# A hybrid decoder layer on one core: the order of work around the fifth attention visit

## The chip, the core and the metric

The kernel runs on one core of one Trainium2 chip. The core has five engines that each work through their own instructions in order: TensorE (PE in the profile, its weight loads PEld), VectorE (DVE), ScalarE (ACT), GpSimd (POOL) and SyncE (SP), which here only issues DMAs. Matmuls write PSUM banks of 128 partitions x 512 f32; everything else lives in SBUF. Engines wait for each other by semaphores. The metric is the device time of one execution, in microseconds (us); less is better.

## The reference, cut to what matters

One layer of a decoder trunk, 256 tokens, width 1024, float32. One combined projection of the normed input feeds two kinds of heads; both outputs go through w_out, then a gated feed-forward part follows.

```python
proj = rms_norm(x, attn_norm_g) @ w_in
y_moba = merge_heads(moba_attention(rope(mq), rope(mk), mv))     # 8 heads of 64, causal
log_a  = log_sigmoid(gate_lr @ w_gate_up + b_gate) / 16
og     = gla_attention(gq, gk, gv, log_a)                        # 4 heads, keys 64, values 128, chunks of 64
og     = og * rsqrt(mean(og * og) + EPS) * gla_norm_g
y_gla  = merge_heads(og) * silu(gr)
x = x + concat([y_moba, y_gla]) @ w_out
h = causal_dwconv(rms_norm(x, ffn_norm_g) @ w_ffn_up, conv_w, conv_b)
x = x + (silu(h_gate) * h_val) @ w_ffn_down
out = rms_norm(x, final_norm_g)
```

With 256 tokens there is one key block, so the first kind of head ("m_" in the code) is plain causal softmax attention.

## The kernel before

**Matmuls in three parts.** Every f32 weight is split by ACT into a rounded part `hi` (L99) and by DVE into the rest `lo` (L102); activations are split likewise (`mh`, `ml`). A product is three matmuls (`mm3`, L115 to L118). Weights come in slots of 128x2048: slots 0 to 15 are w_in, 16 to 19 w_out (L141 to L143), then the up-projection. `raw` has a ring of 4 buffers, `hi` and `lo` of 3. In the plan, `(hi, n, p)` and `(lo, n, p)` split half p (1024 columns) of slot n. `lo` of a slot's last piece issues the DMA of a later slot (`load_next`, L103), on SP's queue.

**Steps and visits.** The projection runs as steps q = 0 to 47, each one group of columns and one slice of k: v is in steps 24 to 31, gv in 32 to 39, r (the gate) in 40 to 47; a step of these is two times three matmuls of 512 columns, for two token tiles. Steps 48 to 63 are the output projection: phase 0 (48 to 55) takes the heads' half y_moba with slots 16 and 17, phase 1 (56 to 63) y_gla with slots 18 and 19; each step makes 128 output columns j with 12 matmuls of 256 columns. The attention's work is put into this stream by a table (L669 to L692): `on(q, f)` runs f ahead of step q, and at q + 0.5 in its middle. What f emits lands on each engine's queue in the order written, so **the table sets the order of work on PE, ACT and DVE at once**. The attention visits PE four times for scores (29, 33.5, 36.5, 40.5); the fifth visit, at 45.5, is what the change's name speaks of.

**What the names do.** `m_scores(pr)` makes scores of two heads in two PSUM banks (and the products of GLA level pr + 2 beside them); `m_max`, `m_exp`, `m_div` (L586 to L608) are the softmax on DVE and ACT, the last of them dividing by the sums: reciprocals on DVE (L603), a 128-wide scale on ACT (L604), a 256-wide one on ACT (L606) or DVE (L608). Heads 0 to 3 are transposed on DVE (`p_blocks`, L566) and by 20 small DMAs into `pt4` (`p_turn`, L569 to L584, on SP's and POOL's queues by turns); heads 4 to 7 on PE into two PSUM banks, from which ACT copies `pt` (`m_pt`, L610 to L625). `lvl_u`, `lvl_u64` (L365) and `lvl_d_` (L402) build GLA's inner products level by level into `ATd`; `lvl_join` (L416) copies them to `AT` on ACT; `lvl_last` (L420) makes the last products on PE, `lvl_last_d` (L438) reads them on ACT. `mv_evac` and `gv_evac` (L523, L448) take v and gv out of PSUM on ACT. `m_av` (L627) and `g_av` (L454) are the products with the values; `m_av` ends with `mh`/`ml` (L643, L645). `g_tail` (L481) norms GLA's output and gates it with silu(r): L471, L477, L452, L491. `g_out` (L493) turns the result on PE (L499) and splits it (L503, L504).

**PSUM banks.** Two pools of four: `acc` for the projections, `att` for the attention, each handed out in turn. `m_av(0)` gets the `att` bank that the first half of `m_pt(3)` wrote, `m_av(1)` the second; `m_pt(3)` gets the banks of `m_scores(3)`, which `lvl_d_(5)` reads last. The output projection's four banks are, in turn, those of gv (two) and those of r (two); output column j uses bank j % 4.

Of the kernel before, what the change touches and what calls it, by code (L numbers as in the profile page):

```python
# [34 lines left out]
def trunk_kernel(ctx: ExitStack, tc: tile.TileContext, xT_d, wG_d, w5_d, wo_d, up_d, dn_d,  # L35
# [79 lines left out]
    def mm3(out, sh, sl, mh, ml, first, last, **kw):  # L115
        T.matmul(out, sh, mh, start=first, stop=False, **kw)  # L116
        T.matmul(out, sh, ml, start=False, stop=False, **kw)  # L117
        T.matmul(out, sl, mh, start=False, stop=last, **kw)  # L118
# [482 lines left out]
    def m_div(h):  # L601
        mx, pe = st["mx", h], st["pe", h]
        V.reciprocal(mx[:, 6:8], mx[:, 4:6])  # L603
        A.activation(pe[:, 0:128], pe[:, 0:128], AF.Copy, scale=mx[:, 6:7])  # L604
        if h in (2, 3, 4, 5):
            A.activation(pe[:, 128:384], pe[:, 128:384], AF.Copy, scale=mx[:, 7:8])  # L606
        else:
            V.tensor_scalar(pe[:, 128:384], pe[:, 128:384], mx[:, 7:8], None, op0=ALU.mult)  # L608
# [41 lines left out]
    def on(q, f, *a):  # L650
        plan.setdefault(q, []).append((f, a))
# [11 lines left out]
    def do(*fs):  # L663
        for f, *a in fs:
            f(*a)
# [3 lines left out]
    for q, f in (  # L669
            (2, lambda: do((xsplit, 6), (xsplit, 7), (xsq, 3), (galloc, 6), (ghi, 6), (glo, 6), (ghi, 7), (glo, 7))),  # L670
            (4, lambda: do((xadd, 3), (xsum,), (hi, 6, 0), (lo, 6, 0), (g_wgs_hi,), (hi, 7, 0))),
            (12, lambda: do((xnorm, lambda: slots[7].split_lo(0, 512)), (lambda: slots[7].split_lo(512, 1024),), (g_evac, 0), (g_lr_split,), (g_evac, 1), (g_wgs_lo,), (hi, 7, 1), (lo, 7, 1))),
            (12.5, lambda: do((DMA.dma_start, lvl, lvl_d), (masks,))),
            (13.5, lambda: do((hi, 8, 0))),
            (14.5, lambda: do((g_transpose_lr,), (g_transpose, 0), (g_transpose, 1), (xrow,), (lo, 8, 0), (g_diag,))),
            (15.5, lambda: do((g_gate_mm,), (g_gate,), (hi, 9, 0), (g_decay,), (lo, 9, 0), (hi, 9, 1))),
            (16.5, lambda: do((lvl_u, 0), (lo, 9, 1), (lvl_u, 1))),
            (18, lambda: do((rope_a, 0, 0), (rope_b, 0, 0), (hi, 10, 0), (lo, 10, 0), (rope_a, 0, 1), (rope_b, 0, 1), (hi, 10, 1), (lo, 10, 1))),
            (20, lambda: do((hi, 11, 0), (lo, 11, 0), (hi, 11, 1), (lvl_keep,), (DMA.dma_start, glag, gla_g_d))),
            (24, lambda: do((lvl_u, 2), (rope_a, 1, 0), (rope_b, 1, 0), (lo, 11, 1), (rope_a, 1, 1), (rope_b, 1, 1), (hi, 12, 0), (lo, 12, 0), (g_diag2, 0), (g_diag2, 4))),  # L680
            (29, lambda: do((hi, 12, 1), (lvl_first,), (m_scores, 0), (m_max, 0), (m_exp, 0), (m_max, 1), (m_exp, 1), (lvl_d_, 0), (lvl_d_, 1), (lvl_u, 3), (m_div, 0), (m_div, 1), (lvl_d_, 2), (lo, 12, 1), (hi, 13, 0), (lo, 13, 0))),
            (33.5, lambda: do((hi, 13, 1), (m_scores, 1), (m_max, 2), (m_exp, 2), (m_max, 3), (m_exp, 3), (lvl_u, 4), (m_div, 2), (m_div, 3), (lo, 13, 1), (lvl_d_, 3), (mv_evac, 0), (mv_evac, 1), (hi, 14, 0), (lo, 14, 0))),
            (36.5, lambda: do((hi, 14, 1), (m_scores, 2), (m_max, 4), (m_exp, 4), (m_max, 5), (m_exp, 5), (lvl_u, 5), (m_div, 4), (m_div, 5), (lvl_d_, 4), (p_blocks,), (p_turn,), (lo, 14, 1))),
            (37, lambda: do((hi, 15, 0))),
            (40.5, lambda: do((hi, 15, 1), (m_scores, 3), (m_pt, 2), (m_max, 6), (m_exp, 6), (m_max, 7), (m_exp, 7), (lo, 15, 0), (lvl_u64,), (lvl_d_, 5), (m_div, 6), (m_div, 7), (lvl_join,), (lo, 15, 1))),
            (41, lambda: do((gv_evac, 0), (gv_evac, 1), (hi, 16, 0), (lo, 16, 0))),
            (42, lambda: do((hi, 16, 1), (lo, 16, 1))),
            (45.5, lambda: do((m_pt, 3), (lvl_last,), (lvl_last_d,), (m_av, 0), (m_av, 1), (g_av, 0), (g_av, 1), (hi, 17, 0), (lo, 17, 0), (hi, 17, 1), (lo, 17, 1))),
            (48, lambda: do((g_tail,), (hi, 18, 0), (lo, 18, 0), (hi, 18, 1), (lo, 18, 1))),
            (51, lambda: do((g_out,),)),  # L690
            (52, lambda: do((A.preload_act_table_set, "abs_reciprocal_sqrt_and_small"), (hi, 19, 0), (lo, 19, 0), (hi, 19, 1), (lo, 19, 1)))):
        on(q, f)  # L692

# [49 lines left out]
    def emit(q):  # L743
        for f, a in plan.get(q, []):
            f(*a)
# [53 lines left out]
    def hsum(n):  # L799
        V.tensor_add(sqs[:, 0:2], sqs[:, 0:2], sqs[:, n:n + 2])  # L800

    for q in range(48, 64):
        ph, j = divmod(q - 48, 8)
        emit(q)
        if q == 56:
            ctx.enter_context(tc.manual_schedule())
        o = wacc[j % 4][:, (j // 4) * S:(j // 4 + 1) * S]
        h_, l_ = slots[16 + 2 * ph + j // 4].view(512)
        cs = slice((j % 4) * 128, (j % 4 + 1) * 128)
        for kk in range(4):  # L810
            if kk == 2:
                emit(q + 0.5)
            k = 4 * ph + kk
            mm3(o, h_[:, kk, cs], l_[:, kk, cs], st["mh"][:, k], ml[:, k],
                ph == 0 and kk == 0 and j < 4, ph == 1 and kk == 3, skip_group_check=True)
        if ph == 1:
            if j == 0:
                ap_.close()
                ff = ctx.enter_context(tc.tile_pool(name="ffn", bufs=1, reuse_waits="tile"))
                sqs = ff.tile([128, KT, S], F32, name="sqs", tag="big")  # L820
            if j % 4 == 0:
                ups[j // 4].alloc()
            hT = xT
            piece = (j % 4 * 512, j % 4 * 512 + 512) if j < 6 else None
            if piece:
                ups[j // 4].split_hi(*piece)
            V.tensor_add(hT[:, j], o, xT[:, j])
            A.activation(hh_[:, j], hT[:, j], AF.Copy, scale=par[:, P_FG + j:P_FG + j + 1])
            if piece:
                ups[j // 4].split_lo(*piece)  # L830
            V.scalar_tensor_tensor(hl_[:, j], hT[:, j], par[:, P_FG + j:P_FG + j + 1], hh_[:, j],
                                   op0=ALU.mult, op1=ALU.subtract)
            if j in (4, 6):
                hsum(j - 2)
            A.activation(sqs[:, j], hT[:, j], AF.Square)
# [377 lines left out]
```

## Time and profile before

| | |
|---|---|
| median of three timed runs | 309.67 us (309.52 to 310.79) |
| the profiled execution | 309.44 us, of it span 307.7 us |
| granted TensorE clock, mean | 0.991 |
| PE waiting for ACT at L637 | 2.9 us, once |
| ACT waiting for PE at L99 | 31.2 us, 11 times |
| DMA over the span | 57.10 MB, mean 186 GB/s |

The span runs from the first to the last instruction; the rest of the execution's time lies around it. Times in the rows below count from the span's start. A row of the timeline has the start, the duration, the engine, the line, the operation, the tiles written and read, and in brackets how long the engine had been idle and what released it; `x4` merges four instructions. `PEclk` is the granted TensorE clock as a share of full speed.

### The profile page before, as it was taken

How to read it: one execution, taken by the hardware profiler on the slowest of the kernel's cores; microseconds unless marked ns; L12 is line 12 of the kernel's file. 1: busy time of each engine (PE TensorE's matmuls, PEld its weight loads, DVE VectorE, ACT ScalarE, POOL GpSimd, SP SyncE). 2: the span in 40 equal slices, each digit the busy share in tenths (PEclk: the TensorE clock that was granted, in tenths of full speed). 3: DMA queues.
4: the chain of work that ended last, by engine and by line, in shares of the span. 5: the costliest groups of instructions: out<-in, count | busy, mean ns of one | idle time of the engine just before them, and what ended most of it. 6: DMA issues, size and time to landing. Idle time of an engine off the chain costs nothing.

```text
span 307.7 us, 6219 instructions
## 1 busy us (share of the span) xinstructions
PE 297.8 (97%) x2446; PEld 282.0 (92%) x2446; DVE 249.7 (81%) x464; ACT 207.0 (67%) x382; POOL 11.0 (4%) x31
## 2 busy tenths in 40 slices
PE   8999999999699999999999999999999999999992
PEld 8999988778489999999999999999999999999991
DVE  3888989969568498799999998888887788876652
ACT  4988999797978487667766776555566655534362
POOL 3010100007000000000000000000000000000000
PEclk9999999999989999999999999999999999999998
DMA  6997745254753533892666666548787722220003
GB/s 177 389 343 307 293 165 218 91 197 77 255 184 135 228 112 136 333 413 75 208 214 229 260 236 232 190 163 225 199 221 230 273 70 68 68 70 0 2 11 126
DMA packets 24188, 57.10 MB, mean 186 GB/s; under 512 B 12976, under 2 KB 14848, under 8 KB 19936
## 3 DMA queue, kind: packets, MB, share of 16 engines
q1 hardware_dynamic: 23696, 56.22, 52.2%
q0 software_dynamic: 320, 0.36, 0.6%
q8 instruction: 19, 0.31, 0.4%
q10 hardware_dynamic: 144, 0.13, 0.1%
q14 instruction: 9, 0.07, 0.1%
HBM read 53.89 MB, written 1.05 MB: 179 GB/s over the span
## 4 chain that ended last, share of the span: by engine, by line
PE 77%; ACT 9%; DVE 8%; issue 3%; DMA 1%; SPq 0%; DVEq 0%; ACTq 0%
PE att L116 14%; PE att L117 14%; PE att L118 14%; PE acc L116 9%; PE acc L117 9%; PE acc L118 9%; PE att L784 3%; DVE lo L102 3%; ACT hi L99 3%; ACT qs L512 2%; PE acc L765 1%; DMA raw<-in_w 1%; PE att L637 1%; DVE ATd L409 1%; DVE pe L590 1%
## 5 line engine op out<-in xcount | busy, mean ns | idle before, releaser
L102 DVE TENSOR_TENSOR lo<-raw,hi 128x1024 fp32r<-128x1024 f32 (+4 forms) x89 | 93.6, 1066 | 15.0 <-ACT hi L99 14.7
L99 ACT ACTIVATE hi<-raw 128x1024 fp32r<-128x1024 f32 (+4 forms) x87 | 79.9, 942 | 37.1 <-PE att L117 31.2
L116 PE MATMUL att<-hh,hi 128*128 128x256 f32 x352 | 98.4, 279 | 0.0
L117 PE MATMUL att<-hl,hi 128*128 128x256 f32 x352 | 98.3, 279 | 0.0
L118 PE MATMUL att<-hh,lo 128*128 128x256 f32 x352 | 98.2, 279 | 0.0
L116 PEld LDWEIGHTS att<-hh,hi 128*128 128x128 f32 x352 | 66.2, 188 | 0.0
L117 PEld LDWEIGHTS att<-hl,hi 128*128 128x128 f32 x352 | 66.2, 188 | 0.0
L118 PEld LDWEIGHTS att<-hh,lo 128*128 128x128 f32 x352 | 66.2, 188 | 0.0
L911 DVE SCALAR_TENSOR_TENSOR c<-us,par,c 128x256 f32<-128x256 f32 x88 | 40.7, 482 | 4.1 <-ACT c L903 2.5
L903 ACT ACTIVATE c<-us,par 128x256 f32<-128x256 f32 x44 | 24.0, 591 | 24.4 <-DVE us L893 18.9
L118 PE MATMUL acc<-dhi,gl 128*128 128x512 f32 (+1 forms) x88 | 32.2, 365 | 0.0
L117 PE MATMUL acc<-dlo,gh 128*128 128x512 f32 (+1 forms) x88 | 32.2, 365 | 0.0
L116 PE MATMUL acc<-dhi,gh 128*128 128x512 f32 (+1 forms) x88 | 31.9, 363 | 0.0
L853 DVE TENSOR_TENSOR dlo<-draw,dhi 128x1024 fp32r<-128x1024 f32 x22 | 26.7, 1219 | 0.0
L848 ACT ACTIVATE dhi<-draw 128x1024 fp32r<-128x1024 f32 x22 | 23.0, 1046 | 0.0
L893 DVE TENSOR_TENSOR us<-att,rb 128x512 f32<-128x512 f32 x20 | 13.8, 689 | 11.2 <-PE att L118 11.2
L116 PE MATMUL acc<-hi,ah 128*128 128x512 f32 x48 | 19.5, 406 | 0.0
L118 PE MATMUL acc<-hi,al 128*128 128x512 f32 x48 | 19.0, 396 | 0.0
L117 PE MATMUL acc<-lo,ah 128*128 128x512 f32 x48 | 19.0, 395 | 0.0
L117 PEld LDWEIGHTS acc<-dlo,gh 128*128 128x128 f32 x88 | 16.5, 188 | 2.0
L116 PEld LDWEIGHTS acc<-dhi,gh 128*128 128x128 f32 x88 | 16.5, 188 | 1.9
L118 PEld LDWEIGHTS acc<-dhi,gl 128*128 128x128 f32 x88 | 16.5, 187 | 1.9
(236 smaller groups left out, 517.5 us busy)
## 6 DMA issues: line engine op xcount, KB each, us to landing
raw<-in_up SPq DMA_DIRECT2D x22, 1024.0 KB, 5.0
draw<-in_dn SPq DMA_DIRECT2D x22, 512.0 KB, 5.7
raw<-in_w SPq DMA_DIRECT2D x7, 1024.0 KB, 6.0
raw<-in_wo SPq DMA_DIRECT2D x4, 1024.0 KB, 6.6
raw<-in_w SPq DMA_DIRECT2D x4, 512.0 KB, 6.4
raw<-in_wG SPq DMA_DIRECT2D x3, 528.0 KB, 5.2
raw<-in_w SPq DMA_DIRECT2D x4, 256.0 KB, 4.9
xg<-hB SPq DMA_DIRECT2D x16, 64.0 KB, 6.1
```

Source lines behind the costliest of these rows:

```text
L99: A.activation(self.hi[:, a:b], self.raw[:, a:b], AF.Copy)
L102: V.tensor_sub(self.lo[:, a:b], self.raw[:, a:b], self.hi[:, a:b])
L116: T.matmul(out, sh, mh, start=first, stop=False, **kw)
L117: T.matmul(out, sh, ml, start=False, stop=False, **kw)
L118: T.matmul(out, sl, mh, start=False, stop=last, **kw)
L512: A.activation(qs[a:a + 32], st["qk"[which]][n][b:b + 32], AF.Copy)
L784: T.matmul(st["G"][tt][c][:, :c1 - c0], sta[:, k, tt * 128:(tt + 1) * 128], mov[:, kk, c0:c1], start=k == 0 and i == 0, stop=k == KT - 1 a ...
L848: A.activation(hi, downs[i][0], AF.Copy)
L853: V.tensor_sub(lo, d, hi)
L893: V.tensor_tensor(u[:, :, 2:], upo[i][2].rearrange("p (a t) -> p a t", a=2), rb[:, None, :].to_broadcast([128, 2, S]), op=ALU.mult)
L903: A.activation(cv[i][:, a], u[:, a, 2:], AF.Identity, bias=par[:, P_CB + m:P_CB + m + 1], scale=par[:, P_CW + 2 * 2 * NP + m:P_CW + 2 * 2 ...
L911: V.scalar_tensor_tensor(c[:, a], u[:, a, w:w + S], par[:, wc:wc + 1], c[:, a], op0=ALU.mult, op1=ALU.add)
```

## The change

The table's entries from 33.5 to 51 get another order, the 256-wide division of heads 6 and 7 goes from DVE to ACT, and phase 0 of the output projection takes its output columns in the order 0, 1, 4, 5, 2, 3, 6, 7.

```diff
-        if h in (2, 3, 4, 5):
+        if h >= 2:
             A.activation(pe[:, 128:384], pe[:, 128:384], AF.Copy, scale=mx[:, 7:8])
...
-            (33.5, lambda: do((hi, 13, 1), (m_scores, 1), (m_max, 2), (m_exp, 2), (m_max, 3), (m_exp, 3), (lvl_u, 4), (m_div, 2), (m_div, 3), (lo, 13, 1), (lvl_d_, 3), (mv_evac, 0), (mv_evac, 1), (hi, 14, 0), (lo, 14, 0))),
-            (36.5, lambda: do((hi, 14, 1), (m_scores, 2), (m_max, 4), (m_exp, 4), (m_max, 5), (m_exp, 5), (lvl_u, 5), (m_div, 4), (m_div, 5), (lvl_d_, 4), (p_blocks,), (p_turn,), (lo, 14, 1))),
+            (33.5, lambda: do((hi, 13, 1), (m_scores, 1), (m_max, 2), (m_exp, 2), (m_max, 3), (m_exp, 3), (lvl_u, 4), (m_div, 2), (m_div, 3), (lo, 13, 1), (lvl_d_, 3), (hi, 14, 0), (lo, 14, 0))),
+            (36.5, lambda: do((hi, 14, 1), (mv_evac, 0), (mv_evac, 1), (m_scores, 2), (m_max, 4), (m_exp, 4), (m_max, 5), (m_exp, 5), (lvl_u, 5), (m_div, 4), (m_div, 5), (lvl_d_, 4), (p_blocks,), (p_turn,), (lo, 14, 1))),
             (37, lambda: do((hi, 15, 0))),
-            (40.5, lambda: do((hi, 15, 1), (m_scores, 3), (m_pt, 2), (m_max, 6), (m_exp, 6), (m_max, 7), (m_exp, 7), (lo, 15, 0), (lvl_u64,), (lvl_d_, 5), (m_div, 6), (m_div, 7), (lvl_join,), (lo, 15, 1))),
-            (41, lambda: do((gv_evac, 0), (gv_evac, 1), (hi, 16, 0), (lo, 16, 0))),
-            (42, lambda: do((hi, 16, 1), (lo, 16, 1))),
-            (45.5, lambda: do((m_pt, 3), (lvl_last,), (lvl_last_d,), (m_av, 0), (m_av, 1), (g_av, 0), (g_av, 1), (hi, 17, 0), (lo, 17, 0), (hi, 17, 1), (lo, 17, 1))),
+            (40.5, lambda: do((hi, 15, 1), (m_scores, 3), (m_pt, 2), (m_max, 6), (m_exp, 6), (m_max, 7), (m_exp, 7), (lo, 15, 0), (m_div, 6), (m_div, 7), (lo, 15, 1), (lvl_u64,), (lvl_d_, 5))),
+            (41, lambda: do((gv_evac, 0), (gv_evac, 1), (lvl_join,))),
+            (46, lambda: do((m_pt, 3), (lvl_last,), (lvl_last_d,), (hi, 16, 0), (lo, 16, 0), (m_av, 0), (m_av, 1), (hi, 16, 1), (lo, 16, 1), (g_av, 0), (g_av, 1), (hi, 17, 0), (lo, 17, 0), (hi, 17, 1), (lo, 17, 1))),
             (48, lambda: do((g_tail,), (hi, 18, 0), (lo, 18, 0), (hi, 18, 1), (lo, 18, 1))),
-            (51, lambda: do((g_out,),)),
+            (51.5, lambda: do((g_out,),)),
...
     for q in range(48, 64):
         ph, j = divmod(q - 48, 8)
+        j = j if ph else (0, 1, 4, 5, 2, 3, 6, 7)[j]
```

On ACT, between the exponentials of heads 6 and 7 and the copies out of m_pt(3)'s banks (L623), the rows are these (- before, + with the change; L604 and L606 divide, L449 is gv_evac, L417 and L418 are lvl_join, L99 is hi of slot 16):

```order
 L597 ACTIVATE pe_152,mx<-pe_152,mx 128x256
-L604 ACTIVATE pe_152<-pe_152,mx 128x128 x2
+L604 ACTIVATE pe_152<-pe_152,mx 128x128
+L606 ACTIVATE pe_152<-pe_152,mx 128x256
+L604 ACTIVATE pe_152<-pe_152,mx 128x128
+L606 ACTIVATE pe_152<-pe_152,mx 128x256
+L449 ACTIVATE gv<-acc,rsx 128x512 x2
 L417 ACTIVATE ATf<-ATd 64x8x64
 L418 ACTIVATE ATf<-ATd 64x8x64
-L449 ACTIVATE gv<-acc,rsx 128x512 x2
-L99 ACTIVATE hi<-raw 128x1024 x2
 L623 ACTIVATE pt<-att 128x2x64
```

Two 256-wide divisions came to ACT, gv's evacuation went ahead of the join, and both halves of hi(16) left; they now stand behind lvl_last_d, the second of them behind mh.

On DVE, behind the maxima of heads 6 and 7 (L590), the first L102 is lo(15,0), the second lo(15,1), and L368, L369 begin lvl_u64:

```order
 L590 ISA mx 128x1
 L102 TENSOR_TENSOR lo<-raw,hi 128x1024
+L603 RECIPROCAL mx<-mx 128x2 x2
+L102 TENSOR_TENSOR lo<-raw,hi 128x1024
 L368 TENSOR_TENSOR gqT<-gqT,dec_132 128x8x32
 L369 TENSOR_TENSOR gkT<-gkT,dec_132 128x8x32
```

The reciprocals came from behind the last masks to directly behind lo(15,0), and lo(15,1) from behind the divisions to behind the reciprocals.

On PE, between g_av and g_out, L116 to L118 with `acc<-hi,ah` are the projection and with `acc<-mh,hi` the output projection:

```order
 L117 MATMUL acc<-lo,ah 128x512
 L118 MATMUL acc<-hi,al 128x512
-L116 MATMUL acc<-hi,ah 128x512
-L117 MATMUL acc<-lo,ah 128x512
-L118 MATMUL acc<-hi,al 128x512
+L116 MATMUL acc<-mh,hi 128x256
+L117 MATMUL acc<-ml,hi 128x256
+L118 MATMUL acc<-mh,lo 128x256
+L116 MATMUL acc<-mh,hi 128x256
+L117 MATMUL acc<-ml,hi 128x256
+L118 MATMUL acc<-mh,lo 128x256
```

Three matmuls of the projection left this place; they now run ahead of m_pt(3). Six more of the output projection stand ahead of g_out, which comes half a step later. The new order of output columns does not show in such rows, since all of them read alike.

## The prediction

> **What bounds the kernel now.** I read the page's busy table first, then who waited for whom, then the chain of work that ended last between 66 and 92 us, then the timelines of TensorE (PE), ScalarE (ACT) and VectorE (DVE) around it.
>
> ```profile
> span 307.7 us, 6219 instructions
> PE 297.8 (97%) x2446; PEld 282.0 (92%) x2446; DVE 249.7 (81%) x464; ACT 207.0 (67%) x382; POOL 11.0 (4%) x31
> ```
>
> PE is busy 97% of the span; only what makes PE stand or run slowly is worth anything. The view of waits (idle in total, times, longest) has one long wait of PE in the whole program:
>
> ```profile
> PE att L637 <- ACT pt L624: 2.9, 1, 2.9
> ```
>
> The timeline shows it (start, duration, idle before and what released it). L617 turns the last two heads' probabilities (m_pt(3)), L435 ends lvl_last, L637/L638 are m_av, L463/L461 g_av; L116 then resumes the projection and, from 93.37, the output projection.
>
> ```profile
> 78.27 0.59 PE L617 MATMUL att<-ident,pe 64*128 64x64 f32 x12
> ...
> 79.51 0.22 PE L435 MATMUL att<-q,gkT 64*64 64x64 f32 x2
> 82.65 0.66 PE L637 MATMUL att<-pt,mv 128*64 128x256 f32 x4 [2.92 <-ACT pt L624]
> ...
> 83.35 0.65 PE L637 MATMUL att<-pt,mv 128*64 128x256 f32 x4
> ...
> 86.92 1.32 PE L463 MATMUL att<-gv,ATf 128*128 128x128 f32 x8
> 88.08 0.39 PE L461 MATMUL att<-gv,AT 128*128 128x128 f32 x2
> ...
> 89.79 0.48 PE L116 MATMUL acc<-hi,ah 128*128 128x512 f32 x1
> ...
> 93.37 0.28 PE L116 MATMUL acc<-mh,hi 128*128 128x256 f32 x1
> ...
> 97.66 0.71 PE L499 MATMUL att<-ident,y 64*128 64x64 f32 x16
> ```
>
> The chain says why (start, length, what):
>
> ```profile
> 74.04 1.14 DVE lo L102
> ...
> 76.45 0.41 DVE ATd L409 x2
> ...
> 77.86 0.63 ACT ATf L417
> ...
> 79.14 1.14 ACT gv L449 x2
> 80.28 1.89 ACT hi L99 x2
> 82.17 0.16 ACT pt L623
> 82.33 0.28 ACT pt L624
> ```
>
> m_av(0) takes the PSUM bank that m_pt(3) filled. It comes free when ACT has read it (L623, L624), and ACT, which works in order, first does the join of the masks, gv's evacuation and both halves of hi(16). PE was done with lvl_last at 79.73 (79.51 + 0.22) and stood until 82.65.
>
> The wait has a second price. Four stretches follow; the columns are the length, busy time and instructions of PE, PEld, DVE, ACT and POOL, the granted clock, the DMA share, GB/s:
>
> ```profile
> 77.00:80.40 3.40, 2.73 (x66) 2.01 (x64) 1.88 (x4) 3.30 (x7) 0.46 (x4) 1.00 0.49 79
> 80.40:83.80 3.40, 1.15 (x13) 0.98 (x15) 2.36 (x2) 3.38 (x10) 0.00 (x0) 1.00 0.96 395
> 83.80:87.20 3.40, 3.40 (x23) 2.73 (x20) 0.82 (x3) 1.66 (x8) 0.00 (x0) 0.51 1.00 407
> 87.20:90.60 3.40, 3.40 (x28) 3.26 (x29) 2.69 (x3) 3.37 (x12) 0.00 (x0) 0.99 0.23 89
> ```
>
> PE is idle for 2.25 of the 3.40 us from 80.40, and the next 3.40 run at a granted clock of 0.51. The stretch from 77.00 had 0.67 idle, and the clock stayed at 1.00 behind it.
>
> **The change, part by part.** The sum stands against the profiled execution: 309.44 us, of which the span is 307.7; the median of the three timed runs, 309.67, is 0.23 above it.
>
> *mv's evacuation behind hi(14).* From the timelines of PE and ACT:
>
> ```profile
> 69.39 0.67 PE L398 MATMUL att<-gqT,gkT 64*64 64x32 f32 x32
> ```
>
> ```profile
> 63.09 1.27 ACT L524 ACTIVATE mv<-acc,rsx 128x512 f32<-128x512 f32 x2
> 64.24 2.01 ACT L99 ACTIVATE hi<-raw 128x1024 fp32r<-128x1024 f32 x2
> 66.80 0.40 ACT L597 ACTIVATE e<-e,mx 128x128 f32<-128x128 f32 x1 [0.55 <-DVE mx L590]
> ...
> 76.96 0.88 ACT L604 ACTIVATE pe<-pe,mx 128x128 f32<-128x128 f32 x2 [1.91 <-DVE mx L603]
> ```
>
> With hi(14) first, DVE's lo(14,0) and the maxima behind it start 1.15 us sooner, and ACT's idle 0.55 before the exponentials goes: the exponentials of heads 4 and 5, p_blocks, and the exponentials of heads 6 and 7 all come 0.55 earlier. PE does not wait there, so this earns nothing by itself. ACT has read mv's banks by 66.2 (63.09 + 2.01 + 1.14). PE writes them anew three matmuls ahead of L398 at 69.39, that is at 68.7 (0.239 each: 15 from 89.79 to 93.37), so the later read costs nothing either.
>
> *Divisors behind the exponentials, all on ACT.* Now ACT stands 1.91 us before L604 at 76.96, since the reciprocals are behind the level of 64 and the masks on DVE. What the two forms cost on ACT stands earlier in the chain, for heads 2 and 3:
>
> ```profile
> 61.68 0.29 ACT pe L604
> 61.97 0.40 ACT pe L606
> ```
>
> lo(15,0) ends at 75.18 (74.04 + 1.14), less 0.55 is 74.65; two reciprocals take it to 74.85. ACT's four instructions (two of 0.29, two of 0.40: 1.4) end at 76.2, and gv's evacuation (1.14) at 77.35. DVE meanwhile does lo(15,1) (1.14, to 76.0), the level of 64 (75.18 to 76.45 in the chain, 1.27, to 77.25) and the last masks (0.41, to 77.65). The join waits for these and takes two of 0.63: 78.9. The two 0.40 are new on ACT; they lie in the 1.91 that it now idles. All of this is beside the projection on PE.
>
> *Three matmuls ahead of m_pt(3), hi(16) behind lvl_last_d.* L617 starts 0.7 later, at 79.0, and ends at 79.6. Its banks were read by the last masks until 77.65, so it need not wait. From 79.6 ACT, free since 78.9, reads it (0.16 + 0.28 for the first bank, done at 80.05). lvl_last ends on PE at 80.43 (79.73 + 0.7). So the bank is free 0.4 us before PE asks: **the wait of 2.92 goes**. If ACT were later than I have it, the cover is those 0.4 us and then each us costs one. The three matmuls only change place, and hi(16) goes into ACT's idle time further down.
>
> What is late next? m_av(0) also reads pt4, which the small DMAs of p_turn fill (count, duration, first and last issue; landing):
>
> ```profile
> L584 SPq DMA_DIRECT2D pt<-tb x4: 599/612/624, 74.9 to 77.5; - x4
> DMA to landing us min/median/max: 1.9/2.7/3.7
> ```
>
> The last is issued at 77.5, so it lands between 79.4 and 81.2; 0.55 earlier, since p_blocks is, that is 78.85 to 80.65 against 80.43. The wait is 0 to 0.25, and 0.8 if the DMAs do not come earlier at all. I take 0, by the median (79.65). On SP's queue the next two loads of w_out stand behind these DMAs, and stay there; the load that lo(16) releases leaves later, which is priced below.
>
> *The clock.* m_av is four pieces of 0.70 at full clock (82.65 to 83.35), 2.80. g_av is 24 matmuls of 0.107 (16 from 88.08 to 89.79), 2.57. From 82.65 to 89.79 the two took 7.14, so the slow clock cost 1.77; by the clock itself it is 3.40 x 0.49 = 1.67. I take **1.7**. With at most 0.7 us of idle in it, as in the stretch from 77.00, the clock should hold.
>
> [...]
>
> *The output banks and g_out.* The output projection then starts at 93.37 - 2.92 - 1.7 = 88.8. At 0.119 a matmul (36 from 93.37 to 97.66), three and a half steps of 12 take 5.0: PE comes to g_out, where it now stands, at 93.8. Is y ready? Rows of ACT, then of DVE:
>
> ```profile
> 84.62 0.72 ACT L643 ACTIVATE mh<-att 128x256 fp32r<-128x256 f32 x3
> 87.03 0.60 ACT L643 ACTIVATE mh<-att 128x512 fp32r<-128x512 f32 x1 [1.69 <-PE att L638]
> ...
> 89.41 0.27 ACT L471 ACTIVATE e<-att 128x128 f32<-128x128 f32 x1
> ...
> 94.02 1.26 ACT L452 ACTIVATE gr<-acc,rsx 128x512 f32<-128x512 f32 x2
> ```
>
> ```profile
> 88.60 2.36 DVE L102 TENSOR_TENSOR lo<-raw,hi 128x1024 fp32r<-128x1024 f32 x2 [0.26 <-ACT hi L99]
> ...
> 94.74 1.29 DVE L491 TENSOR_TENSOR y<-y,gr 128x512 f32<-128x512 f32 x2 [0.18 <-ACT gr L452]
> ```
>
> On ACT, L623 at 82.17 to L643 at 84.62 are 2.45; from 79.6 that is 82.1. Then hi(16,0) 0.95, mh 1.3 (0.72 + 0.60), three halves of hi 2.85: L471 at 87.2, against 89.41 now 2.2 earlier. DVE's last lo ends at 82.1 + 0.95 (hi) + 1.14 (lo) + 1.3 (ml, taken like mh) + 3 x 1.14 = 88.9, against 90.96 (88.60 + 2.36) 2.0 earlier. So y is ready at 96.03 (94.74 + 1.29) - 2.0 = 94.0, its first half at 93.4. PE reaches g_out at 93.8, and its first eight turns (0.35) need only the first half: a wait of 0 to 0.3, I take **0.1**. PE's lead was 4.6, that of y is only 2.0: this is the thinnest place. The new order of banks keeps a second wait away: the banks of r are now asked for in the fifth step, at 95.2; without it the third step would ask at 91.6, and ACT frees the first at 92.4 (94.02 + 0.63 - 2.2). The splits of slot 17, wanted at 91.6, end at 88.9.
>
> *Loads and the rest.* The first up-weights are loaded when lo(16) ends, at 86.7 (82.1 + 0.95 + 1.14 + 1.3 + 1.14, rounded), and first used by ACT at the second row:
>
> ```profile
> raw<-in_up SPq DMA_DIRECT2D x22, 1024.0 KB, 5.0
> ```
>
> ```profile
> 105.49 0.63 ACT L99 ACTIVATE hi<-raw 128x512 fp32r<-128x512 f32 x1 [2.67 <-PE acc L117]
> ```
>
> ACT waits there for PE, not for a load; 4.5 earlier is 101.0, 14 us after the issue, against 5.0 to landing. hi(19) must now wait for slot 16 until the end of PE's sixth step, 98.0, and its lo ends at 101.1; PE wants it in the thirteenth, at 106.4. The view of waits has no row of PE behind g_out, so what it wins it keeps.
>
> The sum: 2.92 + 1.7 - 0.1 = **4.5 us**; 309.44 - 4.5 = 304.9, or 305.2 beside the median.
>
> **The rivals.**
> 1. *The wait moves to pt4's DMAs.* For it: the slowest landing, 81.2 unshifted. Price 0.25 to 0.8, no slow clock (0.67 idle left it alone): 305.4 to 306.0. Against it: the median landing.
> 2. *The slow clock stays* though the gap goes, since m_av's narrow matmuls bring it on, not the gap. For it: it set in some 1.2 us after PE had resumed, on L637. Against it: the stretch ahead of it is the only one here with over 2 us of idle. Price 1.7: 306.9. [...]
> 3. *g_out takes over.* If y is not 2.0 but 0 to 1 us earlier, it comes at 95.0 to 96.0; PE waits 0.9 to 1.9 for its second half and, near the top, may lose the clock (1.7): 306.0 to 308.7. For it: hi(16) and hi(17) now stand ahead of the norms without a gap. Against it: the sum above, from rows.
> 4. *Slower.* The same place, one mechanism: ACT, with three of the four halves of hi(16) and hi(17) between m_av and the norms, holds y back beyond where it is now, 96.03. From a gap of 2.8 at g_out (y at 96.9) with two slow stretches behind it (3.4) the loss is 6.2, more than the 4.6 won and the 1.55 of half a per cent: 311.3 and up. Against it: those halves start 2 us earlier than now and are no longer.
> 5. *It does not do what it says:* the join or the reads before m_av stay late, and PE waits as now: 309.7. That takes 2.9 us on ACT or DVE that I overlook.
>
> **How the numbers follow.** Forecast 304.5 to 305.4: 0.68. First rival 0.12, second 0.07, third 0.06, fourth 0.03, fifth 0.04. The likeliest gives 305.2. Forecast and first rival hold 0.80 and reach 306.0; with the price of the clock, the larger of the unknowns, the range is 304.4 to 306.9. Over 0.5% (1.55 us, about what a measurement of this kernel can tell from no change) faster is below 308.1: forecast, first, second and most of the third, 0.92; within it a rest of the third and the fifth, 0.05; slower 0.03.
>
> **What would show it.** In the changed profile: no wait of PE at L637 over 0.3 us; granted clock 1.00 from 80 to 90; the output projection at 88.8 (93.37 now); g_out at 93.8 with under 0.3 idle; the span near 303.2. A wait at L637 put down to a DMA speaks for the first rival, a 0.5 clock without a gap for the second, a wait at L499 for the third. The forecast is wrong if PE's lead at 88.8 is not there, or is gone by 98.

## The result and the profile after

The changed kernel takes 306.07 us, the median of six runs (305.88 to 306.49); the kernel before, run beside it, 309.61 (six runs, 308.54 to 310.79). The ratio is 0.9885, with a 95% interval of 0.9861 to 0.9908: faster by 1.15%, about 3.5 us of the 4.5 that were forecast. The profiled executions took 309.44 and 306.01.

The page of the changed kernel, its span, PE's busy row and the share of each engine in the chain that ended last:

```profile
span 303.9 us, 6219 instructions
...
PE 296.2 (97%) x2446; PEld 280.6 (92%) x2446; DVE 248.6 (82%) x462; ACT 207.7 (68%) x384; POOL 11.5 (4%) x31
...
PE 95%; DMA 1%; ACT 1%; SPq 0%; issue 0%; DVE 0%; ACTq 0%
```

The span is 3.8 us shorter. PE still sets the end, and 95% of the chain is now PE's own work. Its waits (idle in total, times, longest):

```profile
PE att L637 <- ACT pt L624: 0.6, 1, 0.6
PE acc L764 <- ACT hi L99: 0.3, 1, 0.3
```

The wait at L637 fell from 2.9 to 0.6 us; the forecast had it gone. (The 0.3 at L764 lies near 6 us, at the start of the program, far from the change.) The timeline of the changed kernel on PE, ACT and DVE at the places that the prediction named:

```profile
78.98 0.59 PE L617 MATMUL att<-ident,pe 64*128 64x64 f32 x12
...
80.21 0.23 PE L435 MATMUL att<-q,gkT 64*64 64x64 f32 x2
81.01 0.66 PE L637 MATMUL att<-pt,mv 128*64 128x256 f32 x4 [0.58 <-ACT pt L624]
...
81.68 0.65 PE L637 MATMUL att<-pt,mv 128*64 128x256 f32 x4
...
89.36 0.28 PE L116 MATMUL acc<-mh,hi 128*128 128x256 f32 x1
...
94.15 0.28 PE L118 MATMUL acc<-mh,lo 128*128 128x256 f32 x1
94.36 0.71 PE L499 MATMUL att<-ident,y 64*128 64x64 f32 x16
...
78.15 0.63 ACT L418 ACTIVATE ATf<-ATd 64x512 f32<-64x512 f32 x1
79.60 0.28 ACT L623 ACTIVATE pt<-att 128x128 f32<-128x128 f32 x1 [0.81 <-PE att L617]
79.77 0.38 ACT L624 ACTIVATE pt<-att 128x256 f32<-128x256 f32 x1
...
87.22 0.27 ACT L471 ACTIVATE e<-att 128x128 f32<-128x128 f32 x1
...
92.82 1.30 DVE L491 TENSOR_TENSOR y<-y,gr 128x512 f32<-128x512 f32 x2 [0.20 <-ACT gr L452]
...
101.56 0.63 ACT L99 ACTIVATE hi<-raw 128x512 fp32r<-128x512 f32 x1 [0.82 <-PE acc L117]
```

Up to lvl_last (L435) and in ACT's queue the rows are within 0.12 us of the forecast: the join ends at 78.78, ACT then stands 0.81 us for PE (before, PE stood for ACT), and L471 starts at 87.22. From m_av on PE is 0.6 us late. In four stretches the columns are again length, busy time and instructions of PE, PEld, DVE, ACT and POOL, granted clock, DMA share, GB/s:

```profile
77.60:81.00 3.40, 2.83 (x67) 2.10 (x66) 0.00 (x0) 2.56 (x8) 0.10 (x1) 1.00 0.48 103
81.00:84.40 3.40, 3.39 (x37) 3.02 (x38) 1.14 (x1) 3.29 (x11) 0.00 (x0) 1.00 1.00 419
84.40:87.80 3.40, 3.40 (x27) 3.18 (x27) 3.40 (x7) 3.40 (x9) 0.00 (x0) 1.00 0.27 111
87.80:91.20 3.40, 3.40 (x24) 3.08 (x23) 3.26 (x13) 3.11 (x18) 0.00 (x0) 1.00 0.88 311
```

The granted clock stays at 1.00 through m_av and g_av, where it was 0.51 in the kernel before.

Laying the starts of all 2446 matmuls of the two traces side by side gives the account. The changed kernel is level until 77 us, 4.01 us ahead at 93 (4.6 were forecast there), and 3.75 ahead from 126 us to the end. So 0.6 us stayed at m_av and 0.26 were lost again between 95 and 121 us. Of the 3.8 us of span the profiled executions show 3.4 (309.44 to 306.01), since 0.3 us more of the second lies outside its span. The experiments are about these two, about the clock, and about which part of the change does the work.

### The profile page after: what moved, and what is told of

The parts are those of the page before. It is cut to its first block, busy times and chain, and to the rows that moved or that the text cites. A ratio compares the mean times of both kernels' runs of the same rounds, so it can differ in the third digit from the quotient of the medians.

```text
span 303.9 us, 6219 instructions
## 1 busy us (share of the span) xinstructions
PE 296.2 (97%) x2446; PEld 280.6 (92%) x2446; DVE 248.6 (82%) x462; ACT 207.7 (68%) x384; POOL 11.5 (4%) x31
## 3 DMA queue, kind: packets, MB, share of 16 engines
HBM read 53.89 MB, written 1.05 MB: 181 GB/s over the span
## 4 chain that ended last, share of the span: by engine, by line
PE 95%; DMA 1%; ACT 1%; SPq 0%; issue 0%; DVE 0%; ACTq 0%
PE att L116 14%; PE att L117 14%; PE att L118 14%; PE acc L116 14%; PE acc L117 14%; PE acc L118 14%; PE att L783 3%; PE acc L764 1%; DMA raw<-in_w 1%; PE att L398 1%; PE att L535 1%; PE att L463 1%; PE att L637 1%; PE acc L772 1%; PE att L617 0%
## 5 line engine op out<-in xcount | busy, mean ns | idle before, releaser
L102 DVE TENSOR_TENSOR lo<-raw,hi 128x1024 fp32r<-128x1024 f32 (+4 forms) x89 | 93.6, 1066 | 17.8 <-ACT hi L99 17.7
L99 ACT ACTIVATE hi<-raw 128x1024 fp32r<-128x1024 f32 (+4 forms) x87 | 79.9, 941 | 37.7 <-PE att L117 31.6
L116 PE MATMUL att<-hh,hi 128*128 128x256 f32 x352 | 98.4, 280 | 0.0
L118 PE MATMUL att<-hh,lo 128*128 128x256 f32 x352 | 98.2, 279 | 0.0
L116 PEld LDWEIGHTS att<-hh,hi 128*128 128x128 f32 x352 | 66.2, 188 | 0.0
L118 PEld LDWEIGHTS att<-hh,lo 128*128 128x128 f32 x352 | 66.2, 188 | 0.0
L118 PE MATMUL acc<-dhi,gl 128*128 128x512 f32 (+1 forms) x88 | 32.1, 365 | 0.0
L116 PE MATMUL acc<-dhi,gh 128*128 128x512 f32 (+1 forms) x88 | 32.0, 363 | 0.0
L116 PE MATMUL acc<-hi,ah 128*128 128x512 f32 x48 | 19.5, 406 | 0.0
L118 PE MATMUL acc<-hi,al 128*128 128x512 f32 x48 | 19.0, 396 | 0.0
L116 PEld LDWEIGHTS acc<-dhi,gh 128*128 128x128 f32 x88 | 16.5, 188 | 1.9
L118 PEld LDWEIGHTS acc<-dhi,gl 128*128 128x128 f32 x88 | 16.5, 188 | 1.9
```

The lines of the kernel that those rows point to most:

```text
L99: A.activation(self.hi[:, a:b], self.raw[:, a:b], AF.Copy)
L102: V.tensor_sub(self.lo[:, a:b], self.raw[:, a:b], self.hi[:, a:b])
```

## The experiments

Where the name doesn't say otherwise, an edit is made in the changed kernel. Diffs are cut to the tuple that moves. The medians of before beside the three groups of runs were 309.65, 309.71 and 309.76 us.

**What is left at m_av(0).** ACT is not the last: its fourth read of pt's banks, a row behind those shown, ends at 80.6, and the chain of the changed kernel has a piece that nothing explains (start, length, what):

```profile
80.32 0.29 ACT pt L624
80.60 0.41 issue
81.01 0.62 PE att L637 x3
```

By its semaphore events the last of pt4's transfers landed at 79.48. What runs at that time is seen in the view of line L637 (count; shortest, median, longest in ns; first and last start):

```profile
L637 PE MATMUL att<-pt,mv x16: 379/379/430, 81.0 to 83.3; 128*64 128x256 f32 x16
L637 PEldq EVENT_SEMAPHORE  x10: 51/51/51, 80.0 to 81.1; - x10
```

PE's own sequencer works off nine instructions that only wait on semaphores, one every 0.106 us or so from 80.02 to 80.96, the tenth behind them. m_av(0) has to see the landings of the 20 small transfers that fill pt4; these are counted on sixteen semaphores, and each instruction of the row names one or two. (The expectation below takes the sixteen for rings; in the trace each is counted up by sixteen for one whole transfer, and four of them for a second one.) The order of the two m_av was exchanged:

```diff
-(lo, 16, 0), (m_av, 0), (m_av, 1), (hi, 16, 1)
+(lo, 16, 0), (m_av, 1), (m_av, 0), (hi, 16, 1)
```

> The change, with m_av(1) ahead of m_av(0). Theory A: the 0.6 us that PE still waits at L637 is its own queue, nine semaphore-only instructions of about 0.106 us each, because m_av(0) must see all 16 rings of the pt4 DMAs; m_av(1) needs none of them, so they run while m_av(1) executes. Wait at L637 at most 0.2 us, output projection starts 0.4 to 0.5 earlier than in the change, time about 305.6. Theory B: the wait is for ACT's reads, as the profile's label says; m_av(1) needs a later read than m_av(0), so the wait stays at 0.6 or grows, time 306.1 or more.

Measured: 305.49 us (305.41 to 306.89), ratio 0.9875 (0.9841 to 0.9909). The wait is gone from the list of PE's waits; the timeline of PE has m_av(1) straight behind lvl_last, and the view of the line has the semaphore instructions later:

```profile
80.65 0.23 PE L435 MATMUL att<-q,gkT 64*64 64x64 f32 x2
80.80 0.66 PE L637 MATMUL att<-pt,mv 128*64 128x256 f32 x4
```

```profile
L637 PEldq EVENT_SEMAPHORE  x9: 51/51/51, 80.5 to 81.8; - x9
```

The first of the nine now belongs to m_av(1); the other eight run while PE executes m_av(1), and take 0.80 us (81.10 to 81.90) although all of pt4 had landed by 80.04. The matmuls of this execution run 0.44 us behind those of before from 20 us on, far ahead of any edit; here and below, "measured from its start" has such a lag taken off. Measured so, this kernel is 4.62 us ahead of the one before at 93 us, which is 2.92 + 1.7: the two large terms of the forecast are complete once the semaphore instructions are covered.

**The bank order.** The new order of the first eight output columns was taken out:

```diff
-        j = j if ph else (0, 1, 4, 5, 2, 3, 6, 7)[j]
```

> The change, with the output columns of phase 0 in the old order 0 to 7. Theory: PE asks for r's first bank in its third step, at about 92.2, and ACT frees it at 92.7: a wait of 0.5 us, time about 306.6. Rival: the order earns nothing, no wait there, time 306.1. Beside it: if the 0.27 us that the change loses between 98 and 126 us comes from the order of the banks, it is gone here.

Measured: 307.11 us (306.6 to 307.16), ratio 0.9911 (0.9879 to 0.9944). The waits of PE have the row that was expected of the natural order:

```profile
PE att L637 <- ACT pt L624: 0.6, 1, 0.6
PE acc L116 <- ACT gr L452: 0.5, 1, 0.5
```

So the order of the change is worth its place: from the start of one matmul to the next, this wait sets PE back by 0.76 us. But the loss of 0.26 us between 95 and 121 us is gone in this kernel, which ends 0.50 us behind the changed one, each measured from its start; so the new order also costs something. Two rows each of the timelines of PE show it, of the changed kernel and then of the last kernel of this part; between the two rows lie 170 and 171 steps from matmul to matmul:

```profile
100.06 0.28 PE L116 MATMUL acc<-mh,hi 128*128 128x256 f32 x1
...
120.08 0.28 PE L118 MATMUL att<-hh,lo 128*128 128x256 f32 x1
```

```profile
100.07 0.28 PE L116 MATMUL acc<-mh,hi 128*128 128x256 f32 x1
...
120.03 0.28 PE L116 MATMUL att<-hh,hi 128*128 128x256 f32 x1
```

20.02 us by 170 are 117.8 ns, 19.96 by 171 are 116.7 ns. The slower step starts behind g_out, at 95 us, and ends at two matmuls of L864 at 121.3; from 90 to 93.5 us, in the new order and ahead of g_out, it is 116.7 ns. To see whether the place of g_out sets it, g_out was moved to a whole step:

```diff
-(51.5, lambda: do((g_out,),)),
+(52, lambda: do((g_out,),)),
```

> The changed kernel with g_out at 52 instead of 51.5, so that the 16 transposes no longer stand in the middle of one bank's sum. In the changed kernel matmuls take 117.8 ns instead of 116.7 ns from the end of g_out (95 us) until the L864 matmuls (121.3 us), 0.27 us in all. Theory A (the slower rhythm is set by the place at which PE takes up the output projection again behind g_out): it is gone or starts 0.7 us later, and with it gone the end is 0.2 to 0.3 us earlier, 305.7 to 305.9 us. Theory B (it belongs to the bank order 0, 1, 4, 5, 2, 3, 6, 7 itself): 117.7 to 117.9 ns until 121 us as before, 306.0 to 306.2 us.

Measured: 306.26 us (305.7 to 306.73), ratio 0.9898 (0.9859 to 0.9938). The step is 116.7 ns in the 3.6 us ahead of g_out, which now comes at 95.30, and 117.8 from 96 to 120: the slower rhythm begins behind g_out at its new place too, and stays. Theory A's promise, a gain, failed; the place only moves the beginning. Last, another order that also asks late for the banks of r, in the kernel with the exchanged m_av:

```diff
-        j = j if ph else (0, 1, 4, 5, 2, 3, 6, 7)[j]
+        j = j if ph else (0, 4, 1, 5, 2, 6, 3, 7)[j]
```

> The change with m_av(1) ahead of m_av(0), and the output columns of phase 0 in the order 0, 4, 1, 5, 2, 6, 3, 7. r's banks are asked for in the fifth step as in the change, slot 17 from the second step on (at about 90.8, its splits end at 89.2). If the 0.26 us lost between 98 and 126 us belongs to the order 0, 1, 4, 5, it is gone: 0.26 less than the swap alone, about 305.2; if it belongs to any order but the old one, it stays, 305.5.

Measured: 305.29 us (305.01 to 305.59), ratio 0.9861 (0.9839 to 0.9883), span 303.0, no wait of PE at r's banks, 116.7 ns throughout, and 4.61 us ahead, measured from the start, from 93 us to the end. All its runs lie below all those of the changed kernel (305.88 to 306.49), which were taken in another group of runs; the intervals of the two ratios overlap. That the step depends on the order of the columns is shown by two pairs of kernels that differ in the order alone, and the other profiles agree: from 100 to 118 us the step is 117.8 ns in all eight kernels with the order 0, 1, 4, 5, 2, 3, 6, 7 and 116.7 in the five with another. Why a sequence of matmuls with the same operands and shapes takes 1% longer behind g_out isn't shown.

**The splits of 16 and 17.** First those of 16 went back ahead of m_pt(3), then those of 17 as well, then those of 16 and half of 17:

```diff
-(gv_evac, 1), (lvl_join,))),
+(gv_evac, 1), (lvl_join,), (hi, 16, 0), (lo, 16, 0), (hi, 16, 1), (lo, 16, 1))),
...
-(46, lambda: do((m_pt, 3), (lvl_last,), (lvl_last_d,), (hi, 16, 0), (lo, 16, 0), (m_av, 0), (m_av, 1), (hi, 16, 1), (lo, 16, 1), (g_av, 0)
+(46, lambda: do((m_pt, 3), (lvl_last,), (lvl_last_d,), (m_av, 0), (m_av, 1), (g_av, 0)
```

> The change, with both halves of hi(16) and lo(16) back ahead of m_pt(3), behind the join. Theory: the other reorderings already brought ACT's reads forward; ACT ends the join at 78.8, hi(16) at 80.7, the first bank is read at 81.1 and the wait at L637 is about 0.8 instead of 0.6, clock 1.00: time about 306.3. Rival: the place of hi(16) is what took the wait away: wait about 2.5 and a halved clock, time near 309.7.

Measured: 306.62 us (306.31 to 306.74), ratio 0.9902 (0.9867 to 0.9937), a wait of 0.7 at L637, a mean granted clock of 0.994 to 0.997. With the rest of the change in place, the splits of 16 are not needed to take the wait away.

> The change, with hi and lo of slots 16 and 17 all ahead of m_pt(3): 3.8 us of ACT in front of the reads, so a gap of about 2.6 us at L637, with the rest of the change in place. Theory: a gap of this size halves the clock for one stretch of 3.4 us (1.7 lost): 2.0 + 1.7 more than the change, about 309.8. [...]

Measured: 309.82 us (308.29 to 310.14), ratio 0.9996 (0.9967 to 1.0025), a wait of 2.6: with 17 ahead as well, the whole gain is gone. Seven of its ten executions have a mean granted clock of 0.989 to 0.992 (0.990 the profiled one, with its stretch at 0.51), and three of 0.996 or 0.997.

> The change, with hi(16) and the first half of hi(17) ahead of m_pt(3): 2.85 us of ACT in front of the reads, a gap of about 1.7 us at L637. [...]

Measured: 307.69 us (307.21 to 308.62), ratio 0.9943 (0.9912 to 0.9973), a wait of 1.6. These two bracket the clock. The stretches at the wait and behind it, first with the wait of 2.6, then with that of 1.6:

```profile
79.60:83.00 3.40, 1.42 (x61) 1.21 (x60) 2.68 (x3) 3.40 (x4) 0.10 (x1) 1.00 0.80 257
83.00:86.40 3.40, 2.80 (x18) 2.16 (x20) 1.95 (x2) 2.60 (x11) 0.00 (x0) 0.51 1.02 429
```

```profile
79.96:83.37 3.41, 1.77 (x64) 1.44 (x61) 3.07 (x3) 3.40 (x9) 0.10 (x1) 1.00 0.81 291
...
83.37:86.78 3.41, 3.41 (x40) 3.11 (x36) 1.85 (x5) 3.13 (x10) 0.00 (x0) 1.00 1.01 425
```

With PE idle for 1.98 of 3.40 us the next stretch was granted 0.51; with 1.64 of 3.41, the whole gap, it was granted 1.00. None of the six executions of the second kernel lost clock (0.993 to 0.996 over the whole run). Two of them took 308.5 and 308.6 us all the same, which the clock does not explain.

**One part alone.** Three kernels ask which parts carry the gain. In the kernel before, only the splits of 16 were moved behind lvl_last_d:

```diff
-(gv_evac, 1), (hi, 16, 0), (lo, 16, 0))),
-(42, lambda: do((hi, 16, 1), (lo, 16, 1))),
+(gv_evac, 1))),
...
-(lvl_last_d,), (m_av, 0), (m_av, 1), (g_av, 0)
+(lvl_last_d,), (hi, 16, 0), (lo, 16, 0), (m_av, 0), (m_av, 1), (hi, 16, 1), (lo, 16, 1), (g_av, 0)
```

> The kernel before, with only hi(16) and lo(16) moved behind lvl_last_d as in the change. By ACT alone the first bank is read at 80.7 and the wait at L637 would be 1.0 instead of 2.9. Theory: pt4's last DMA, which landed at 81.16 in the profile of before behind a fetch of instructions, is next, and behind it PE's own semaphore instructions: wait 1.0 to 1.9, clock mostly held, time about 307 to 308. Rival: hi(16) is the whole cause, wait at most 0.6, time 306.1.

Measured: 306.56 us (306.39 to 306.89), ratio 0.9901 (0.9872 to 0.9931): nearly the gain of the whole change, from the one move. The wait of PE is

```profile
PE att L637 <- ACT pt L624: 1.4, 1, 1.4
```

and the clock is 1.00 from 76.97 to 83.80; that is 2.9 - 1.4 + 1.7 = 3.2, and the span is 2.8 shorter in an execution whose matmuls run 0.33 us later from 20 us on (3.07 from its start). Of the sixteen parts of pt4's last transfer one landed at 80.88, 1.3 us behind the other fifteen, and the semaphore instruction that looks for it ran at 80.91, three more behind it. So here the first rival is paid: ACT alone explains a wait of about 1.05 (2.92 less the 1.87 by which it comes sooner to L623).

Then, in the kernel before, only the divisors and the join (lvl_join goes behind gv_evac too):

```diff
-        if h in (2, 3, 4, 5):
+        if h >= 2:
...
-(lo, 15, 0), (lvl_u64,), (lvl_d_, 5), (m_div, 6), (m_div, 7), (lvl_join,), (lo, 15, 1))),
+(lo, 15, 0), (m_div, 6), (m_div, 7), (lo, 15, 1), (lvl_u64,), (lvl_d_, 5))),
```

> The kernel before with one part of the change alone: the last two divisions and the join in the new order (the division of heads 6 and 7 on ACT, the join behind gv). The hi parts of tile 16 stay ahead of m_pt(3), the visit stays at 45.5, the banks in natural order. Theory (the wait at m_av(0) is ACT's lateness, and gaps of up to 1.6 us do not halve the clock): ACT reaches pt's bank 1.5 us earlier than in the kernel before (80.55 against 82.07 us in the run with the splits of 16 ahead), so the wait falls from 2.92 to about 1.4 us and the halved clock goes: 2.92 - 1.4 + 1.7 = 3.2 us in the trace, 306.2 to 306.7 us. Rival (the divisors are worth little by themselves, the splits have to move): the wait stays above 2.5 us and the clock halves, 309 us or more.

Measured: 309.19 us (307.47 to 309.66), ratio 0.9966 (0.994 to 0.9992), a wait of 2.1, and the clock halves in the profile (seven of its ten executions have 0.989 to 0.991 over the whole run, three 0.994 to 0.996). The expectation failed, and the rival was nearer. I had taken ACT's gain from the run with the splits of 16 back, which has mv's evacuation behind hi(14) as well. ACT's timelines show what that does, of the kernel before, of that run and of this one, first an exponential of head 6, then the first read of pt's bank:

```profile
73.18 0.40 ACT L597 ACTIVATE pe<-pe,mx 128x128 f32<-128x128 f32 x1 [0.38 <-DVE mx L590]
...
82.07 0.26 ACT L623 ACTIVATE pt<-att 128x128 f32<-128x128 f32 x1
```

```profile
72.72 0.40 ACT L597 ACTIVATE pe<-pe,mx 128x128 f32<-128x128 f32 x1 [0.31 <-DVE mx L590]
...
80.77 0.25 ACT L623 ACTIVATE pt<-att 128x128 f32<-128x128 f32 x1
```

```profile
73.44 0.40 ACT L597 ACTIVATE pe<-pe,mx 128x128 f32<-128x128 f32 x1 [0.38 <-DVE mx L590]
...
81.48 0.25 ACT L623 ACTIVATE pt<-att 128x128 f32<-128x128 f32 x1
```

Less the 0.22 and 0.25 us by which the matmuls of these two executions run later, the exponential comes at 72.50 in the run with mv's evacuation moved and at 73.19 without it, and L623 at 80.55 and 81.23. So the divisors and the join make ACT 0.84 us earlier, not 1.5; the other 0.7 came from mv's place (0.55 in the prediction). The stretches of this kernel fit those above, 2.07 of 3.41 us idle and then half the clock:

```profile
79.03:82.44 3.41, 1.34 (x56) 1.12 (x54) 1.78 (x2) 3.40 (x9) 0.10 (x1) 1.00 0.56 145
82.44:85.85 3.41, 3.41 (x26) 2.72 (x24) 1.04 (x3) 2.34 (x9) 0.00 (x0) 0.50 0.99 420
```

Third and fourth, mv's evacuation went back ahead of hi(14) in the changed kernel, and the visit from 46 back to 45.5:

```diff
-(lvl_d_, 3), (hi, 14, 0), (lo, 14, 0))),
+(lvl_d_, 3), (mv_evac, 0), (mv_evac, 1), (hi, 14, 0), (lo, 14, 0))),
...
-(hi, 14, 1), (mv_evac, 0), (mv_evac, 1), (m_scores, 2)
+(hi, 14, 1), (m_scores, 2)
```

> The change, with mv's evacuation back ahead of hi(14). Theory: ACT, DVE and p_turn come 0.55 us later, and ACT has 0.81 idle before L623 to take it up; pt4's last landing moves from 79.5 to 80.0, PE looks at that semaphore at 80.6: no loss, 306.1, wait at L637 0.6. Rival: the 0.55 comes through to the end: 306.6; or pt4's last landing meets the instruction fetch that PE causes near 79.9 and the wait grows to 1.2 or more.

Measured: 306.53 us (306.09 to 306.69), ratio 0.9898 (0.9873 to 0.9923), a wait of 0.5. By the median the rival's number came, but not by the trace: this execution's matmuls run 0.70 us later from 20 us on, long before the edit, and measured from its start it is 3.78 us ahead at the end, against 3.75 of the changed kernel. The instruction fetch of the second rival did not meet pt4's landing: the 16 KB packet of the instruction queue came at 77.2 us here, and at 75.9 in the changed kernel. That PE causes this fetch, no trace shows.

```diff
-(46, lambda: do((m_pt, 3)
+(45.5, lambda: do((m_pt, 3)
```

> The changed kernel with the visit back at 45.5 instead of 46, nothing else. PE then comes to L617 0.7 us earlier, while ACT's queue is as it was (join until 78.8 us, L604 to L606, gv and join without a split ahead of pt). Theory: ACT is free before PE is done either way (its last read ends 0.9 us before m_av(0) starts), so the wait at m_av(0) is PE's row of semaphore instructions again, plus at most 0.5 us for the join that L617 or the pt reads now meet: the end comes out within 0.5 us of the changed kernel's, 306.0 to 306.6 us. Rival (the half step of the visit is what took the wait away): a wait of 1.3 us or more at m_av(0), 306.8 us or more.

Measured: 306.52 us (305.89 to 306.98), ratio 0.9904 (0.9872 to 0.9935), a wait of 0.6 again, 3.77 us ahead measured from the start. By the traces each of these two parts is worth nothing while the others stand; the medians, of four and five runs that spread over 0.6 and 1.1 us, could not tell 0.5 us.

One sum holds the waits at L637 together. Of 2.92 us of lateness ACT gains 1.87 by the splits of 16, 0.84 by divisors and join and 0.7 by mv's place, and PE comes to m_av 0.7 later by the visit: 4.1 in all. With the splits of 16 back, 2.92 - 0.84 - 0.7 - 0.7 gives 0.7, as measured; the divisors alone leave 2.1, as measured. The 0.84 and the 0.7 were read off ACT's rows of these same two runs, so that the sums close says only that the wait in both is ACT's lateness. Two other runs test it: the splits of 17 put 0.95 and 1.9 us more of ACT in front, and the waits grew from 0.7 to 1.6 and 2.6. Where the parts exceed 2.92, the semaphore instructions leave 0.5 to 0.6.

## Why the prediction was right, and where its sizes were off

The forecast was right in sign, place and mechanism. The time of 306.07 is 0.9 us above the predicted 305.2 and inside the range, but above the likeliest stretch, 304.5 to 305.4; it stands at the upper end of what was given to the first rival. Point by point:

- **PE is the bound, and the one long wait is worth having.** Right. The two kernels that leave a wait of 2 us or more (309.82 and 309.19) gain nothing or little, the one that leaves 1.6 stands at 307.7, and all that leave 1.4 or less lie between 305.3 and 307.2.
- **"The wait of 2.92 goes"**: mis-sized. 0.58 us stayed. ACT freed the first bank at 80.15 (80.05 by the forecast) and the last transfer of pt4 landed at 79.48, ahead of PE; but PE's sequencer needed until 80.96 for its semaphore instructions. The exchange of m_av(0) and m_av(1) shows it. In the kernel before they were hidden behind ACT's lateness (they ran from 79.32 to 81.56, and ACT's read of the bank ended at 82.61), and the prediction asked which engine or transfer would be late next, but not what PE itself does ahead of m_av(0).
- **pt4's last transfer, 79.65 by the median.** The landing at 79.48 is near it by luck. The last issue did not come 0.55 us sooner: it began at 77.6 us (77.5 before), since the one ahead of it took 1.5 us on SP instead of 0.6, and it landed after 1.84 us. In the kernel before it took 3.6 us and landed at 81.16, so with ACT on time PE would have waited for it. Why that issue took 1.5 us is open. The row of the changed kernel (count; shortest, median, longest in ns; first and last start):

```profile
L584 SPq DMA_DIRECT2D pt<-tb x4: 599/610/1504, 74.1 to 77.6; - x4
```

- **The clock, 1.7 us.** Right in mechanism: half clock came with the gap (0.51 behind 2.92 us) and went with it (1.00 behind 0.58). In size it holds for the profiled execution, but not every execution pays it. Of 43 executions of the kernel before that ran beside the experiments, 11 had a mean granted clock of 0.993 or more and a median of 308.2 us, the other 32 of 309.9: the same 1.7 us, in three executions of four. The median of all 43 is 309.7.
- **g_out, 0.1.** Right, and the thinnest place held. y was ready at 94.12 (92.82 + 1.30), 0.1 us behind the forecast, and the list of waits has no row there. But PE came at 94.36 instead of 93.8, held up at m_av, so this run alone doesn't test it. The kernel with the exchanged m_av and the order 0, 4, 1, 5 does: PE came at 93.72, y was ready at 93.92, and PE did not wait, since its first eight turns need only the first half of y.
- **The new order of banks.** It keeps away the wait at r's banks, as said (0.5 us with the natural order). That it would also slow the matmuls behind g_out by 1%, 0.27 us, no term had.
- **Divisors, splits, three matmuls ahead of m_pt(3), mv.** The places came out (L617 at 78.98, the join until 78.78, L471 at 87.22). But the sum treated them as one cover, and the runs show that it is larger than needed: ACT now idles 0.81 us ahead of L623. mv's move earns PE nothing here, as forecast; its 0.7 on ACT counts only where ACT is still late.
- **Loads and hi(19).** hi(19) starts at 98.73 and is no wait of PE; the first split of the up-weights comes 3.9 us earlier than before, at 101.56, and waits for PE as before.

The sum with the measured sizes is 2.92 + 1.7 - 0.58 - 0.27 = 3.8 us, as the span lost (307.7 - 303.9).

Of the rivals, the first (pt4's transfers) has the right place and nearly the right price, but not the right cause: the transfers had landed. Its own mechanism shows in the kernel with the splits of 16 moved alone. The second, a slow clock that stays, is refuted: m_av runs at 1.00 in the same narrow matmuls. Gaps of 2.9, 2.6 and 2.1 us had a clock of 0.51, 0.51 and 0.50 behind them here, one of 1.6 had 1.00. The other three did not come.

## What to carry to other kernels

An edit that removes a wait is worth the wait down to whatever is ready second, and that may be the waiting engine's own row of semaphore instructions; with an instruction that waits for fewer things put in front, the row of 0.80 us cost nothing here. In the profiles a gap of PE was paid a second time, by 1.7 us, where PE was idle for 1.98 us or more of a 3.4 us stretch, and not at 1.64 or less, so shortening one from 2.9 to 1.4 us was worth more (3.1 us) than closing the rest. When several moves cover one wait, try each alone: here the splits of one tile brought nearly all of it, the divisors little, and two others nothing beside them.

## What was not expected of the hardware

- The matmul that reads what 20 small transfers have written, counted on sixteen semaphores, has a row of eight or nine semaphore instructions of PE's sequencer ahead of it, some 0.106 us apart: 0.80 us in all behind m_av(1) and 0.93 in the changed kernel, although everything had landed. Behind m_av(1) the row cost PE no time.
- The records of the granted clock: in the kernel before full for 78.51 us from 5.37, half for 3.41 from 83.88, by m_av, and full for 218.45 from 87.29; in the changed kernel full for 296.96 from 3.90. These are 23, 1, 64 and 87 times 3.413 us. Around m_av the lowest idle share that had half clock in the next stretch was 0.58 (1.98 of 3.40), the highest that had full clock 0.48 (1.64 of 3.41); at the end of the changed kernel, where PE runs out of work, PE was idle for 2.97 of 3.41 us from 297.45, and the clock behind it was 0.50. Why 3 of 10 executions with a gap of 2.1 or of 2.6 in the profile, and 11 of 43 with one of 2.9, kept a mean of 0.993 or more was not shown.
- A sequence of matmuls with one shape ran for 26 us at 117.8 ns a step instead of 116.7, by the order of output columns ahead of it. The cause is open.
- One of the sixteen parts of a small transfer landed 1.3 us behind the others (80.88 against 79.56 us, with the splits of 16 moved alone), in the kernel before 1.8 us (81.16 against 79.38).
